# Feature-major queries and keys, and an earlier S5 part, in the first mixer of a two-layer decoder trunk

## Chip, cores and metric

One core of one Trainium2 chip. The metric is the device time in microseconds (us) of one execution. Engines: PE multiplies matrices (PEld is its weight load), DVE, ACT and POOL work element by element, SP issues the loads. Each engine takes its own instructions in the program's order, and waits for others by semaphores.

## What is computed

A trunk of two layers on 256 rows of width 1024, all in float32. The lines that matter here:

```
x = x + 0.5 * swiglu(rmsnorm(x))                      (first feed-forward stage)
proj = rmsnorm(x) @ w_in                              (first mixer)
u, c_q, c_kv, k_rope = split(proj, 512, 384, 256, 32)
s5 = gelu(S5(u)) gated by sigmoid(gelu(S5(u)) @ w_glu + b)
q = rmsnorm(c_q) @ w_uq        8 heads of 64 plain + 32 rotated columns
k, v = rmsnorm(c_kv) @ w_ukv   8 heads of 64 + 64; all heads share the rotated k_rope
o = causal_attention(q, k, v)
x = x + concat(s5, o) @ w_out
x = x + 0.5 * swiglu(...); x = x + 0.5 * swiglu(...)
x = x + differential_attention(rmsnorm(x)); x = x + 0.5 * swiglu(...); rmsnorm(x)
```

S5 is a diagonal state space: per group of 16 channels and each of 64 states a complex recurrence runs over the rows.

## The kernel before

The program runs in stages one after the other: feed-forward 0, first mixer (`mixer0`), feed-forward 1 and 2, second mixer, feed-forward 3, final norm. A build-time scheduler fixes each engine's order from the order of the code and from priorities; at run time nothing is moved.

**Weights.** `Weights` (L31 to L86) loads every weight in pieces of 128 x 1024 (512 KB) through SP into five `stage` buffers. ACT casts a piece to a high half (`whi`, L71), DVE subtracts to get the low half (`wlo`, L72), and each product is three products of halves. `mix0` (L165) is the list in which the first mixer's weights are loaded.

**Feed-forward 0** (`ffn`, L287) goes through 22 chunks `f` of the hidden width. PE computes chunk `f`'s gate and up products (`gu`, L318 in this stage), ACT and DVE make the hidden piece `hs`, and two chunks later PE multiplies it down into `acc` (L335). The hidden pieces of the first two chunks are turned by PE (`hT`, L367), the second of them right after chunk 2. Between the chunks this stage also runs a background generator, four steps a chunk at first, with all that later stages need and that does not depend on x: `rope_tables` (L491; cosines and sines from the positions, by range reduction `rtk`, `rtr` in `sincos`, then eighteen small DVE operations into `cc`, `ss`), the constants of the mixers (`lp`, `le`, `lw`: a scalar of the second mixer, by a power on POOL), and the S5 matrices (`s5_prep`; `w_re`, `w_im`, `tmat`). The lines of `rope_tables` that the change goes on from:

```
for t in range(2):
    for (cc, ss, o, h) in ((cc0, ss0, 0, 16), (cc1, ss1, 16, 8)):
        ...
        nc.vector.tensor_copy(out=cc[:, t, :h], in_=c)
        ...
        nc.vector.tensor_copy(out=ss[:, t, h:], in_=s)
```

**The first mixer** projects in the order queries' latent `cq`, keys' and values' latent `ckv`, S5 input `pu` (L732). Latents are normalised and turned into `cqh`, `cql`, `ckh`, `ckl`. `queries` makes q with the rows on the partitions (`pq`, 384 columns for four heads), POOL rotates 32 columns of each head (`rope`, L520), and `heads_turned` turns every head of q and k by PE (L935, 32 transposes), so that `scores` (L948, L949) can contract over 96 features. `u` is turned and spread into blocks, `block_inputs` (L886, L887) and `states` compute the S5 states on DVE (`z_re`, `z_im`, two scans, `xs_re`) and partly on POOL (`xs_im`, L918), and `outputs` (L991 to L993) makes `yp` from them. `attend(h)` issues the scores of head h + 2, then transposes head h's probabilities (`pt`, L763, copied to `pT` by ACT, L765) and multiplies them with v (`po`). The output products `attended` on `acc` (L743) start after head 6.

## Time and profile before

| | |
|---|---|
| runs | 1046.18, 1046.80, 1046.37 us (median 1046.37) |
| profiled execution | 1037.45 us, of it 1035.7 us span |
| granted clock, mean | 0.984 of full speed |
| PE busy | 1007.7 us (97%) |
| feed-forward 0 | 0 to 227 us |
| first mixer, PE's part | 227.3 us (first transposes of y) to 350.5 us; the gate's product `pz` starts at 327.3 |

The span runs from the first to the last instruction of the profiled execution. All times "at" below are us from its start. Busy time of PE is modelled: what a product costs is read from the distance of starts. An idle time in brackets is that before an instruction on its own engine, with what ended it.

### The profile page before, as it was taken

How to read it: one execution, taken by the hardware profiler on the slowest of the kernel's cores; microseconds unless marked ns; L12 is line 12 of the kernel's file. 1: busy time of each engine (PE TensorE's matmuls, PEld its weight loads, DVE VectorE, ACT ScalarE, POOL GpSimd, SP SyncE). 2: the span in 40 equal slices, each digit the busy share in tenths (PEclk: the TensorE clock that was granted, in tenths of full speed). 3: DMA queues.
4: the chain of work that ended last, by engine and by line, in shares of the span. 5: the costliest groups of instructions: out<-in, count | busy, mean ns of one | idle time of the engine just before them, and what ended most of it. 6: DMA issues, size and time to landing. Idle time of an engine off the chain costs nothing.

```text
span 1035.7 us, 15225 instructions
## 1 busy us (share of the span) xinstructions
PE 1007.7 (97%) x5796; PEld 878.4 (85%) x5796; DVE 677.4 (65%) x1251; ACT 545.3 (53%) x978; POOL 83.8 (8%) x109
## 2 busy tenths in 40 slices
PE   9999997999979999999999999999999999999997
PEld 7999996989868888888888888888888888888885
DVE  5789778366777885555558555554757777655543
ACT  5444442365636665555447455553567766555542
POOL 2110006600520000000000000000001000000000
PEclk9999999899969999999999999999999999999999
DMA  8766663134213596555628655564453448556521
GB/s 261 250 198 189 203 186 120 52 117 169 82 41 96 177 317 204 184 183 183 207 79 266 201 183 184 187 193 147 140 185 115 142 143 294 184 188 192 190 80 41
DMA packets 49802, 174.83 MB, mean 169 GB/s; under 512 B 6081, under 2 KB 7105, under 8 KB 49730
## 3 DMA queue, kind: packets, MB, share of 16 engines
q1 hardware_dynamic: 48576, 170.20, 51.2%
q10 hardware_dynamic: 1154, 3.67, 1.1%
q8 instruction: 45, 0.74, 0.3%
q14 instruction: 27, 0.22, 0.1%
HBM read 172.80 MB, written 1.05 MB: 168 GB/s over the span
## 4 chain that ended last, share of the span: by engine, by line
PE 85%; DVE 7%; ACT 3%; issue 2%; DMA 1%; POOL 1%; POOLq 0%; ACTq 0%; DVEq 0%; SPq 0%
PE acc L335 22%; PE gu L302 21%; PE gu L304 10%; PE gu L318 10%; PE proj L732 6%; PE gt L355 3%; PE acc L743 3%; DVE wlo L72 1%; DMA stage<-in_wff_dram 1%; PE pt L197 1%; PE pu L732 1%; DVE tmat L125 1%; PE ckv L732 1%; PE pz L1024 1%; PE cq L732 1%
## 5 line engine op out<-in xcount | busy, mean ns | idle before, releaser
L72 DVE TENSOR_TENSOR wlo<-stage,whi 128x1024 fp32r<-128x1024 f32 (+1 forms) x236 | 284.2, 1214 | 189.1 <-ACT whi L71 189.0
L302 PE MATMUL gu<-y,whi 128*128 128x512 f32 x960 | 341.6, 398 | 0.0
L71 ACT CAST whi<-stage 128x1024 fp32r<-128x1024 f32 (+1 forms) x236 | 241.0, 1032 | 126.9 <-PE gu L302 67.0
L304 PE MATMUL gu<-y,wlo 128*128 128x256 f32 x960 | 269.5, 281 | 0.0
L302 PEld LDWEIGHTS gu<-y,whi 128*128 128x128 f32 x960 | 180.4, 188 | 43.9
L335 PE MATMUL acc<-dhi,hs 128*128 128x512 f32 x704 | 193.1, 392 | 1.1 <-DVE hs L125 0.8
L304 PEld LDWEIGHTS gu<-y,wlo 128*128 128x128 f32 x960 | 181.4, 189 | 2.1
L335 PEld LDWEIGHTS acc<-dhi,hs 128*128 128x128 f32 x704 | 126.4, 188 | 28.1 <-DVE hs L125 2.3
L71 ACT CAST dhi<-stage 128x1024 fp32r<-128x1024 f32 x88 | 92.1, 1048 | 67.0 <-DMA stage<-in_wff_dram 66.8
L72 DVE TENSOR_TENSOR dlo<-stage,dhi 128x1024 fp32r<-128x1024 f32 x88 | 108.4, 1232 | 22.6 <-ACT dhi L71 22.4
L318 PE MATMUL gu<-y,whi 128*128 128x256 f32 x640 | 117.5, 285 | 0.0
L335 PE MATMUL acc<-dlo,hs 128*128 128x512 f32 x352 | 110.6, 390 | 0.0
L318 PEld LDWEIGHTS gu<-y,whi 128*128 128x128 f32 x640 | 102.0, 194 | 1.3
L318 PE MATMUL gu<-y,wlo 128*128 128x256 f32 x320 | 91.2, 285 | 0.0
L125 DVE TENSOR_TENSOR both<-gu,both 128x256 f32<-128x256 f32 x120 | 50.5, 421 | 47.2 <-ACT both L305 47.2
L305 ACT COPY both<-gu 128x256 f32<-128x256 f32 x120 | 44.4, 370 | 66.4 <-PE gu L304 66.4
L335 PEld LDWEIGHTS acc<-dlo,hs 128*128 128x128 f32 x352 | 66.1, 188 | 14.3
L134 ACT CAST hs<-sh 128x256 fp32r<-128x256 f32 x80 | 32.5, 406 | 66.2 <-DVE sh L125 66.1
L732 PE MATMUL proj<-whi,y 128*128 128x512 f32 x192 | 62.6, 396 | 0.2 <-ACT y L134 0.2
L318 PEld LDWEIGHTS gu<-y,wlo 128*128 128x128 f32 x320 | 62.0, 194 | 0.2 <-DVE wlo L72 0.2
L177 POOL TENSOR_TENSOR rs<-rs,mhalf 128x1 f32<-128x1 f32 x14 | 7.7, 553 | 668.6 <-DVE rs L131 668.6
L355 PE MATMUL gt<-whi,y 128*128 128x256 f32 x256 | 49.9, 289 | 0.8 <-ACT y L134 0.7
(330 smaller groups left out, 1221.5 us busy)
## 6 DMA issues: line engine op xcount, KB each, us to landing
stage<-in_wff_dram SPq DMA_DIRECT2D x264, 512.0 KB, 4.6
stage<-in_w_in_dram SPq DMA_DIRECT2D x24, 512.0 KB, 4.6
stage<-in_w_out_dram SPq DMA_DIRECT2D x16, 512.0 KB, 3.8
gain<-in_gains_dram ACTq DMA_DIRECT2D x6, 512.0 KB, 4.8
stage<-in_w_u_dram SPq DMA_DIRECT2D x4, 512.0 KB, 4.1
xr<-in_x_dram SPq DMA_DIRECT2D x2, 512.0 KB, 5.0
stage<-in_w_cq_dram SPq DMA_DIRECT2D x2, 512.0 KB, 3.7
stage<-in_w_ckv_dram SPq DMA_DIRECT2D x2, 512.0 KB, 4.6
```

The lines of the kernel that those rows point to most:

```text
L71: nc.scalar.copy(out=hi[:, c:c + w], in_=t[:, :w])
L72: nc.vector.tensor_tensor(out=lo[:, c:c + w], in0=t[:, :w], in1=hi[:, c:c + w].bitcast(F32), op=ALU.subtract)
L125: return nc.vector.tensor_tensor(out=out, in0=a, in1=b, op=op)
L134: copy = nc.scalar.copy(out=hi, in_=src)
L302: nc.tensor.matmul(gu, gh[:, k, s, :], y2[:, k].rearrange("p s c -> p (s c)"), start=k == 0, stop=False)
L304: nc.tensor.matmul(gu[:, :SEQ], gl[:, k, s, :], yh[:, k, :], start=False, stop=k == KT - 1)
L305: nc.scalar.copy(out=both[:, s], in_=gu[:, SEQ:])
L318: nc.tensor.matmul(gu[:, s * 256:(s + 1) * 256], w[:, k, s, :], a[:, k, :], start=(k == 0 and n == 0), stop=(k == KT - 1 and n == 2))
L335: nc.tensor.matmul(acc[t][c], a[:, sl], w[:, c * 512:(c + 1) * 512], start=(f == 0 and n == 0), stop=(f == NF - 1 and n == 2))
L355: last = nc.tensor.matmul(o, a[:, k, sl], w[:, k * 256:(k + 1) * 256], start=(k0 == 0 and n == 0), stop=(k0 > 0 and n == 11))
L732: last = nc.tensor.matmul(acc, a[:, k0 + k, sl], w[:, k * width:(k + 1) * width], start=(k0 == 0 and n == 0), stop=(k0 + per == nk and n = ...
L743: mm = nc.tensor.matmul(acc[t][c], a[:, k0 + k, sl], w[:, o:o + 512], start=(first and k == 0 and n == 0), stop=(last and k == 1 and n == 2))
```

## The change

1. **First mixer, u first.** `mix0` and the projections go `u`, `cq`, `ckv`. `u_blocks` runs between the two halves of `cq`, `block_inputs` between those of `ckv`; `states` has more stops (`step`), which are spread between the later parts, and `xs_im` is computed on DVE.
2. **Feature-major queries and keys.** The query weights are cut at 768 columns and each head is padded from 96 to 128 columns: 64 plain, 32 rotated, and the same 32 with halves swapped (three casts and three subtractions a piece). `queries` and `keys` produce features on the partitions, 256 rows wide; one DVE multiplication by a table `qtab` of ones, cosines and sines does the rotation, and the scores contract over 128. `heads_turned` goes, as do the rotations on POOL; the shared key part is rotated once on POOL (`key_rotation`) and turned (two transposes of `kd`).
3. **The table.** `rope_tables` ends with two DVE copies into `ct`, two PE transposes of it and an ACT copy into `qtab`.
4. **Attention's output products** are issued in four parts between heads 4 to 7; `attend` transposes head h before it issues the next scores; `gelu` is cut in two.

```diff
+    @staticmethod
+    def step(spec):
+        return 768 if spec[1] == "queries" else 1024
...
-                                    op=ALU.subtract)
+            parts = [(hi[:, c:c + w], lo[:, c:c + w], t[:, :w])]
+            if wide == "queries":
+
+                rows = slice(c // 96, (c + w) // 96)
+                h, l = (a[:, :1536].rearrange("p (r d) -> p r d", d=128)[:, rows] for a in (hi, lo))
+                v = t[:, :w].rearrange("p (r d) -> p r d", d=96)
+                parts = [(h[:, :, :96], l[:, :, :96], v)]
+                parts += [(h[:, :, a:a + 16], l[:, :, a:a + 16], v[:, :, b:b + 16]) for a, b in ((96, 80), (112, 64))]
+            for h, l, v in parts:
+                nc.scalar.copy(out=h, in_=v)
+                nc.vector.tensor_tensor(out=l, in0=v, in1=h.bitcast(F32), op=ALU.subtract)
...
-    mix0 = [(w, True) for w in (w_cq[0], w_cq[1], w_ckv[0], w_ckv[1], w_u[0], w_u[1], w_uq[0], w_ukv[0], w_uq[1],
-                                w_ukv[1], w_out0[2], w_glu, w_out0[3], w_out0[0], w_out0[1])]
+    mix0 = [(w, True) for w in (w_u[0], w_u[1], w_cq[0], w_cq[1], w_ckv[0], w_ckv[1])]
+    mix0 += [(w_uq[0], "queries"), (w_ukv[0], True), (w_uq[1], "queries"), (w_ukv[1], True)]
+    mix0 += [(w, True) for w in (w_out0[2], w_glu, w_out0[3], w_out0[0], w_out0[1])]
...
+        ct = s2("ct", [128, 2, 128])
+        nc.gpsimd.memset(ct[:, :, :64], 1.0)
+        nc.vector.tensor_copy(out=ct[:, :, 64:96], in_=cc0)
+        nc.vector.tensor_copy(out=ct[:, :, 96:], in_=ss0)
+        pt = bank("pt")[:, :SEQ]
+        for t in range(2):
+            nc.tensor.transpose(pt[:, t * 128:(t + 1) * 128], ct[:, t], ident)
+        nc.scalar.copy(out=qtab, in_=pt)
...
-        cq = [bank("cq")[:, :384] for _ in range(2)]
+
+        pu = [bank("pu") for _ in range(2)]
         c0, c1 = queue.pop(0), queue.pop(0)
-        product(cq[0], 0, c0, 0, 4, 384, yh, yl, KT)
+        product(pu[0], 0, c0, 0, 4, 512, yh, yl, KT)
         finish()
...
-        def project(acc, width, between):
-            for b in range(2):
-                w = queue.pop(0)
-                for t in range(2):
-                    product(acc[t], t, w, 4 * b, 4, width, yh, yl, KT)
-                more()
-                if b == 0:
-                    between()
...
-        ckv = [bank("ckv")[:, :288] for _ in range(2)]
-        project(ckv, 288, lambda: None)
-        cky = [low_rank(ckv[t][:, :256], 256, qg[:, 384:]) for t in range(2)]
...
-        def latents():
-            for t in range(2):
-                transpose_split(cqy[t], 3, cqh, cql, t)
-            for t in range(2):
-                transpose_split(cky[t], 2, ckh, ckl, t)
-
-        project(pu, 512, latents)
...
+        def project(acc, b, width):
+            w = queue.pop(0)
+            for t in range(2):
+                product(acc[t], t, w, 4 * b, 4, width, yh, yl, KT)
+            more()
...
+            kd, a, b = (s2(n, [128, 2, m]) for n, m in (("kd", 128), ("ka", 32), ("kb", 32)))
...
+            op(a, kp, cc0, MUL)
+            op(b[:, :, :16], kp[:, :, 16:], ss0[:, :, :16], MUL)
+            op(b[:, :, 16:], kp[:, :, :16], ss0[:, :, 16:], MUL)
+            op(kd[:, :, 64:96], a, b, ADD)
+            nc.gpsimd.tensor_copy(out=kd[:, :, 96:], in_=kd[:, :, 64:96])
+            return kd
...
         def queries(g):
-            w = queue.pop(0)
-            h = slice(4 * g, 4 * g + 4)
-            pq = [bank("pq")[:, :384] for _ in range(2)]
+
+            wh, wl = (w[:, :1536].rearrange("p (k h d) -> p k h d", k=3, h=4) for w in queue.pop(0))
+            for b in range(2):
+                pq = bank("pq").rearrange("p (h c) -> p h c", h=2)
+                for j in range(2):
+                    for n, (k, w, a) in enumerate(highs_first(range(3), wh, wl, cqh, cql)):
+                        nc.tensor.matmul(pq[:, j], w[:, k, 2 * b + j], a[:, k, :], start=n == 0, stop=n == 8)
+                h = 4 * g + 2 * b
+                tt(qT[:, h:h + 2, :], pq, qtab.unsqueeze(1).to_broadcast([128, 2, SEQ]), MUL)
+            more()
...
+        def keys(g):
...
+            for j in range(2):
+                for n, (k, w, a) in enumerate(highs_first(range(2), wh, wl, ckh, ckl)):
+                    nc.tensor.matmul(pk[:, j], w[:, k, 0, 128 * j:128 * j + 128], a[:, k, :], start=n == 0,
+                                     stop=n == 5)
+            for r in range(2):
+                nc.scalar.copy(out=kT[:64, 4 * g + r:4 * g + 4:2, :], in_=pk[64 * r:64 * r + 64])
...
+        def key_values(g):
...
             for t in range(2):
-                product(pq[t], t, w, 0, 3, 384, cqh, cql, 3)
-                nc.scalar.copy(out=q_sb[t][:, h, :], in_=pq[t].rearrange("p (h d) -> p h d", h=4))
-                rope(q_sb[t][:, h, 64:96], 4, cc0[:, t, :], ss0[:, t, :], 16, nc.gpsimd)
...
-        def keys_values(g):
...
-                product(pk[t].rearrange("p s c -> p (s c)"), t, w, 0, 2, 512, ckh, ckl, 2)
-                nc.scalar.copy(out=kfull[t][:, h, 0:64], in_=pk[t][:, 0].rearrange("p (h d) -> p h d", h=4))
-                nc.scalar.copy(out=v_sb[:, t, 256 * g:256 * g + 256], in_=pk[t][:, 1])
...
-        queries(0)
-        for t in range(2):
-            kv = kpe[:, t:t + 1, :]
-            rope(kv, 1, cc0[:, t, :], ss0[:, t, :], 16, nc.gpsimd)
-            nc.gpsimd.tensor_copy(out=kfull[t][:, :, 64:96], in_=kv.to_broadcast([128, 8, 32]))
...
-        keys_values(0)
+                sl = slice(t * 128, (t + 1) * 128)
+                for n, (k, w, a) in enumerate(highs_first(range(2), wh, wl, ckh, ckl)):
+                    nc.tensor.matmul(pv[:, t], a[:, k, sl], w[:, k, 1, :], start=n == 0, stop=n == 5)
+            nc.scalar.copy(out=v_sb[:, :, 256 * g:256 * g + 256], in_=pv)
+            more()
...
+            for z, x, y, op in ((z_re, v_re, v_im, ADD), (z_im, v_im, v_re, SUB)):
+                tt(z, x, c, MUL)
+                tt(t1, y, s, MUL)
+                tt(z, z, t1, op)
+                yield
             scan(z_re)
...
-            t2 = s2("t2", sh)[:, :, a]
-            for out, x, y, op in ((xs_im[:, h, o], z_re[:, :, a], s[:, :, a], MUL), (t2, z_im[:, :, a], c[:, :, a], MUL),
-                                  (xs_im[:, h, o], xs_im[:, h, o], t2, ADD)):
-                nc.gpsimd.tensor_tensor(out=out, in0=x, in1=y, op=op)
-
-        v = [block_inputs(b) for b in range(2)]
-        st = [states(b, *v[b]) for b in range(2)]
+            for xs, x, y, op in ((xs_re, z_re, z_im, SUB), (xs_im, z_im, z_re, ADD)):
...
+        def step(b):
+            next(st[b], None)
+
+        cq, ckv = ([bank(n)[:, :w] for _ in range(2)] for n, w in (("cq", 384), ("ckv", 288)))
+        project(cq, 0, 384)
+        u_blocks()
+        project(cq, 1, 384)
+        cqy = [low_rank(cq[t], 384, qg[:, :384]) for t in range(2)]
+        project(ckv, 0, 288)
+        st.append(states(0, *block_inputs(0)))
+        step(0)
+        project(ckv, 1, 288)
+        cky = [low_rank(ckv[t][:, :256], 256, qg[:, 384:]) for t in range(2)]
+        kd = key_rotation()
+        for t in range(2):
+            transpose_split(cqy[t], 3, cqh, cql, t)
+        step(0)
+        st.append(states(1, *block_inputs(1)))
...
-        def heads_turned(g):
-            for t in range(2):
-                for src, dst in ((q_sb, qT), (kfull, kT)):
-                    pt = bank("pt").rearrange("p (k c) -> p k c", c=128)
-                    for k in range(4):
-                        nc.tensor.transpose(pt[:96, k, :], src[t][:, 4 * g + k, :], ident)
-                    d = dst[:96, 4 * g:4 * g + 4, t * 128:(t + 1) * 128]
-                    if src is q_sb:
-                        nc.vector.tensor_copy(out=d, in_=pt[:96])
-                    else:
-                        nc.scalar.copy(out=d, in_=pt[:96])
-
...
-            nc.tensor.matmul(sp[:, :128], qT[:96, h, :128], kT[:96, h, :128], start=True, stop=True)
-            nc.tensor.matmul(sp[:, 128:384], qT[:96, h, 128:], kT[:96, h, :], start=True, stop=True)
+            nc.tensor.matmul(sp[:, :128], qT[:, h, :128], kT[:, h, :128], start=True, stop=True)
+            nc.tensor.matmul(sp[:, 128:384], qT[:, h, 128:], kT[:, h, :], start=True, stop=True)
...
+        def attended(w, t, k0, start, ks=(0, 1)):
+            if start and 0 in ks:
                 acc[t] = [bank("acc") for _ in range(2)]
-            out_product(acc, t, w, oh, ol, k0, start, False)
...
         def attend(h):
+            pT = turned(sc.pop(h), pb)
             if h < 6:
                 sc[h + 2] = scores(h + 2)
-            values(h, sc.pop(h))
...
-        heads_turned(0)
-        sc = {0: scores(0), 1: scores(1)}
-        next(st[0])
+            values(h, pT)
...
+        queries(0)
...
+        pt = bank("pt")[:, :SEQ]
+        for t in range(2):
+            nc.tensor.transpose(pt[:, t * 128:(t + 1) * 128], kd[:, t], ident)
...
+        step(1)
+        keys(0)
+        step(0)
+        key_values(0)
+        sc[0], sc[1] = scores(0), scores(1)
+        step(1)
+        step(0)
         queries(1)
+        step(0)
         attend(0)
-        next(st[1])
-        keys_values(1)
+        step(1)
+        keys(1)
+        key_values(1)
         attend(1)
-        for _ in st[0]:
-            pass
-        heads_turned(1)
-        for _ in st[1]:
-            pass
-        more()
+        step(1)
         yp = outputs(0)
         attend(2)
...
+        step(1)
         attend(3)
         osb = normalised(0)
-        attend(4)
+        g0 = gelu(yp)
         yp = outputs(1)
         heads_out(0, osb)
-        more()
+        attend(4)
+        w2 = queue.pop(0)
+        attended(w2, 0, 0, True, (0,))
+        in_channels(0, g0)
         attend(5)
-        gelu(1, yp)
+        attended(w2, 0, 0, True, (1,))
+        g1 = gelu(yp)
+        attend(6)
+        attended(w2, 1, 0, True, (0,))
+        in_channels(1, g1)
+        attend(7)
         halves(gh, gl, gt)
-        attend(6)
-        w2 = queue.pop(0)
-        attended(w2, 0, 0, True)
-        attend(7)
-        attended(w2, 1, 0, True)
-        heads_out(1, normalised(1))
+        attended(w2, 1, 0, True, (1,))
+        osb = normalised(1)
+        heads_out(1, osb)
         more()
         glu()
         w = queue.pop(0)
```

**Where instructions stand.** PE around chunk 2's turn in feed-forward 0, before (`hT` is the turn, the `gu` ahead of it ends chunk 2, that behind it begins chunk 3):

```order
L318 MATMUL gu<-y_121,wlo 128x256
L367 MATMUL hT<-ident,he 128x128 [waits DVE_49]
L367 MATMUL hT<-ident,he 128x128
L318 MATMUL gu<-y_121,whi 128x256 [waits Activation_49]
L318 MATMUL gu<-y_121,whi 128x256
```

and in the change (L380 is L367 of before, L331 is L318):

```order
L331 MATMUL gu<-y_122,wlo 128x256
L380 MATMUL hT<-ident,he 128x128 [waits DVE_49]
L380 MATMUL hT<-ident,he 128x128
L534 MATMUL pt<-ident,ct 128x128 [waits DVE_49,Pool_49]
L534 MATMUL pt<-ident,ct 128x128
L331 MATMUL gu<-y_122,whi 128x256 [waits Activation_49]
L331 MATMUL gu<-y_122,whi 128x256
```

The two transposes of `ct` stand between the turn and chunk 3's first product, with a wait for DVE and one for POOL.

DVE at the table's steps, before (`sh` and `hs` belong to chunk 3, `rtk` and `rtr` to the tables' range reduction):

```order
L131 TENSOR_SCALAR rtkh<-rtkh 128x48 [waits DVE_49]
L125 TENSOR_TENSOR sh<-sh,gu 128x256 [waits Activation_49]
L125 TENSOR_TENSOR rtk<-rtk,rtkh 128x48 [waits DVE_49]
L128 SCALAR_TENSOR_TENSOR rtr<-rtkh,ang 128x48
L125 TENSOR_TENSOR le<-lw,lc 128x2 [waits Pool_49]
L72 TENSOR_TENSOR wlo<-stage,whi 128x1024 [waits DMAHW1_49]
L128 SCALAR_TENSOR_TENSOR rtr<-rtk,rtr 128x48 [waits DVE_49]
L125 TENSOR_TENSOR nlam<-le 128x1 [waits DVE_49]
L125 TENSOR_TENSOR hs<-sh,hs 128x256 [waits Activation_49]
L128 SCALAR_TENSOR_TENSOR rtr<-rtkh,rtr 128x48 [waits DVE_49]
```

and in the change, the same stretch, then the end of the tables' steps:

```order
L137 TENSOR_TENSOR rtk<-rtk,rtkh 128x48 [waits DVE_49]
L140 SCALAR_TENSOR_TENSOR rtr<-rtkh,ang 128x48
L137 TENSOR_TENSOR le<-lw,lc 128x2 [waits Pool_49]
L140 SCALAR_TENSOR_TENSOR rtr<-rtk,rtr 128x48 [waits DVE_49]
L137 TENSOR_TENSOR nlam<-le 128x1 [waits DVE_49]
L140 SCALAR_TENSOR_TENSOR rtr<-rtkh,rtr 128x48 [waits DVE_49]
L143 TENSOR_SCALAR nlam<-nlam 128x1 [waits DVE_49]
L140 SCALAR_TENSOR_TENSOR rtr<-rtk,rtr 128x48 [waits DVE_49]
```

```order
L524 COPY cc_98<-co 128x8
L525 COPY cc_98<-co 128x8
L526 TENSOR_SCALAR ss_99<-si 128x8
L527 COPY ss_99<-si 128x8
L530 COPY ct<-cc_96 128x2x32 [waits DVE_49]
L531 COPY ct<-ss_97 128x2x32
L85 TENSOR_TENSOR wlo<-stage,whi 128x1024 [waits DMAHW1_49,PE_49,Activation_49]
L137 TENSOR_TENSOR sh<-sh,gu 128x256 [waits Activation_49]
L85 TENSOR_TENSOR wlo<-stage,whi 128x1024 [waits DMAHW2_49,Activation_49]
L137 TENSOR_TENSOR hs<-sh,hs 128x256 [waits Activation_49]
```

Chunk 3's `sh` and `hs` stood in the middle of the range reduction; now they stand behind all of it, behind the eighteen copies and behind both copies into `ct`.

ACT ahead of the keys' product in the mixer, before (`ckh` is the halved latent from which keys and values are made):

```order
L810 COPY kpe<-ckv 128x32 [waits DVE_49] x2
L71 CAST whi<-stage 128x1024 [waits DMAHW4_49,PE_49,Activation_49]
L71 CAST whi<-stage 128x128 [waits DMAHW5_49]
L134 CAST cqh<-pt 128x3x128 [waits PE_49] x2
L134 CAST ckh<-pt 128x2x128 [waits PE_49] x2
L824 COPY us<-pu 128x512 [waits PE_49]
```

and in the change:

```order
L146 CAST cqh<-pt 128x3x128 [waits PE_49] x2
L856 COPY kp<-ckv 128x32 [waits DVE_49]
L84 CAST whi<-stage 128x8x96 [waits DMAHW7_49,PE_49]
L84 CAST whi<-stage 128x8x16 x2
L84 CAST whi<-stage 128x4x96 [waits DMAHW0_49]
L84 CAST whi<-stage 128x4x16 x2
L146 CAST ckh<-pt 128x2x128 [waits PE_49,Pool_49]
L146 CAST ckh<-pt 128x2x128 [waits PE_49]
```

The six casts of the second query weight have come between `cqh` and `ckh`.

## Rows read from the trace of the kernel before

**Rows 1.** The page, section 1: busy time, share of the span and instructions of each engine
```profile
PE 1007.7 (97%) x5796; PEld 878.4 (85%) x5796; DVE 677.4 (65%) x1251; ACT 545.3 (53%) x978; POOL 83.8 (8%) x109
```

**Rows 2.** Windows; columns: stretch, then busy us of engines, granted clock (PEclk), DMA share, GB/s
```profile
20.00:168.00 148.00, 148.00 (x1066) 139.91 (x1064) 121.58 (x311) 71.57 (x103) 17.77 (x19) 1.00 0.64 200
168.00:178.00 10.00, 3.26 (x17) 2.23 (x15) 10.00 (x8) 0.89 (x2) 9.51 (x6) 0.95 0.52 147
178.00:190.00 12.00, 11.27 (x54) 11.30 (x55) 1.78 (x3) 2.70 (x4) 2.26 (x3) 0.50 0.14 49
293.00:306.00 13.00, 12.52 (x56) 12.24 (x57) 7.81 (x15) 2.84 (x7) 1.53 (x1) 0.50 0.26 82
```

**Rows 3.** Timeline of PE, first feed-forward stage; columns: start us, length us, line, operation
```profile
32.60 0.48 PE L318 MATMUL gu<-y,whi 128*128 128x256 f32 x2
...
34.11 0.40 PE L318 MATMUL gu<-y,whi 128*128 128x256 f32 x2
...
34.47 0.40 PE L318 MATMUL gu<-y,whi 128*128 128x256 f32 x2
```

**Rows 4.** Timeline of DVE beside it; in brackets idle time before and its releaser
```profile
40.71 0.29 DVE L125 TENSOR_TENSOR lp<-lv 128x128 f32<-128x128 f32 x1 [1.49 <-DMA lv<-in_lamv_dram]
...
44.94 0.16 DVE L125 TENSOR_TENSOR le<-lw,lc 128x2 f32<-128x2 f32 x1 [2.62 <-POOL lw L436]
...
50.29 0.17 DVE L128 SCALAR_TENSOR_TENSOR s5r<-s5kh,s5sc 128x16 f32<-128x16 f32 x1
50.49 0.18 DVE L128 SCALAR_TENSOR_TENSOR s5r<-s5k,s5r 128x16 f32<-128x16 f32 x1
...
52.10 0.20 DVE L125 TENSOR_TENSOR co<-co 128x48 f32<-128x48 f32 x1
...
53.43 0.17 DVE L511 COPY ss<-si 128x8 f32<-128x8 f32 x1
...
54.59 0.28 DVE L125 TENSOR_TENSOR s5sc<-s5sc 128x16 f32<-128x16 f32 x2 [0.28 <-ACT s5sc L427]
```

**Rows 5.** Timeline of POOL beside it
```profile
41.27 2.98 POOL L436 TENSOR_TENSOR s5w<-euler,s5t 128x16 f32<-128x16 f32 x1 [19.15 <-DVE s5t L125]
44.22 0.69 POOL L436 TENSOR_TENSOR lw<-euler,le 128x2 f32<-128x2 f32 x1
```

**Rows 6.** Timeline of PE, the products that follow the setup's long waits
```profile
187.47 0.77 PE L318 MATMUL gu<-y,whi 128*128 128x256 f32 x2
...
190.61 0.29 PE L318 MATMUL gu<-y,wlo 128*128 128x256 f32 x1
```

**Rows 7.** Timeline of PE, the mixer's first output product of the S5 part
```profile
287.64 0.43 PE L991 MATMUL yp<-u,tmat 128*128 128x64 f32 x2 [0.47 <-DVE t L125]
293.48 0.69 PE L992 MATMUL yp<-xs_re,w_re 128*128 128x64 f32 x2 [5.40 <-DVE xs_re L125]
...
306.65 0.35 PE L964 MATMUL po<-v_sb,pT 128*128 128x64 f32 x2
```

**Rows 8.** Timeline of PE, queries (pq) and turned heads (L935)
```profile
258.60 0.33 PE L732 MATMUL pq<-whi,cqh 128*128 128x384 f32 x1
...
260.16 1.03 PE L861 MATMUL pt<-ident,us 128*128 128x128 f32 x8
...
271.25 0.60 PE L935 MATMUL pt<-ident,q_sb 128*96 128x128 f32 x4
271.68 0.60 PE L935 MATMUL pt<-ident,kfull 128*96 128x128 f32 x4
```

**Rows 9.** Groups by line and shape, ACT, 225 to 355 us: count, busy us, mean ns
```profile
L71 ACT CAST whi<-stage 128x1024 fp32r<-128x1024 f32 x24 | 24.6, 1047 | 6.3 <-PE ckv L732 2.3 <-PE cq L732 1.6 <-PE pu L732 1.3
L71 ACT CAST whi<-stage 128x128 fp32r<-128x128 f32 x4 | 1.2, 294 | 0.0
```

**Rows 10.** Timeline of DVE in the mixer, a state product beside POOL's and one alone
```profile
285.25 1.74 DVE L125 TENSOR_TENSOR t<-z_im,sinn 128x504 f32<-128x504 f32 x1
...
296.26 0.67 DVE L125 TENSOR_TENSOR t<-z_im,sinn 128x504 f32<-128x504 f32 x1
```

More of the change, by code (lines that the diff above doesn't have):

```diff
@@ L734, in product, with out_product @@
         return last.ins
-    def out_product(acc, t, ws, hi, lo, k0, first, last):
+    def out_product(acc, t, ws, hi, lo, k0, first, last, ks=(0, 1)):
         wh, wl = ws
         sl = slice(t * 128, (t + 1) * 128)
-        for k in range(2):
+        for k in ks:
             for n, (w, a) in enumerate(three(wh, wl, hi, lo)):
@@ L824, in mixer0, with u_blocks @@
             nc.scalar.copy(out=us[t], in_=pu[t])
-        q_sb = [s4("q_sb", [128, 8, 96]) for _ in range(2)]
-        kfull = [s4("kfull", [128, 8, 96]) for _ in range(2)]
+        uT = s4("uT", [128, 4, 4, NBLK])
+        u = s4("u", [128, NPAIR, NBLK])
+        def u_blocks():
+            for t in range(2):
+                pt = bank("pt").rearrange("p (k c) -> p k c", c=128)
+                for k in range(4):
+                    nc.tensor.transpose(pt[:, k, :], us[t][:, k * 128:(k + 1) * 128], ident)
+                pv = pt.rearrange("p m (n i) -> p m i n", i=4)
+                for i in range(4):
+                    nc.scalar.copy(out=uT[:, :, i, 32 * t:32 * t + 32], in_=pv[:, :, i, :])
+            uv = u.rearrange("p (m a) n -> p m a n", a=4)
+            for a in range(4):
+                for i in range(4):
+                    dst = uv[32 * i:32 * i + 32, :, a, :]
+                    src = uT[32 * a:32 * a + 32, :, i, :]
+                    if i == 3 or i == 1 and a % 2:
+                        nc.scalar.copy(out=dst, in_=src)
+                    else:
+                        nc.vector.tensor_copy(out=dst, in_=src)
@@ new lines, in mixer0, with key_rotation, op @@
+        cqh, cql = s4("cqh", [128, 3, SEQ], F32R), s4("cql", [128, 3, SEQ], F32R)
+        ckh, ckl = s2("ckh", [128, 2, SEQ], F32R), s2("ckl", [128, 2, SEQ], F32R)
+        def project(acc, b, width):
[3 more added lines that the diff above has]
+            more()
+        def key_rotation():
+            kd, a, b = (s2(n, [128, 2, m]) for n, m in (("kd", 128), ("ka", 32), ("kb", 32)))
+            kp = s2("kp", [128, 2, 32])
+            for t in range(2):
+                nc.scalar.copy(out=kp[:, t], in_=ckv[t][:, 256:288])
+            def op(out, x0, x1, o):
+                nc.gpsimd.tensor_tensor(out=out, in0=x0, in1=x1, op=o)
+            nc.gpsimd.memset(kd[:, :, :64], 0.0)
+            op(a, kp, cc0, MUL)
[4 more added lines that the diff above has]
+            return kd
@@ L865, in mixer0 @@
-        u = s4("u", [128, NPAIR, NBLK])
-        uv = u.rearrange("p (m a) n -> p m a n", a=4)
-        for a in range(4):
-            for i in range(4):
-                dst = uv[32 * i:32 * i + 32, :, a, :]
-                src = uT[32 * a:32 * a + 32, :, i, :]
-                if i == 3 or i == 1 and a % 2:
-                    nc.scalar.copy(out=dst, in_=src)
-                else:
-                    nc.vector.tensor_copy(out=dst, in_=src)
-        keys_values(0)
+            wh, wl = (w[:, :1536].rearrange("p (k h d) -> p k h d", k=3, h=4) for w in queue.pop(0))
@@ L955, in scores, with values @@
             return s
-        def values(h, s):
+        def values(h, pT):
             g, k = divmod(h, 4)
@@ L994, in outputs, with gelu, in_channels @@
             return yp
-        def gelu(b, yp):
-            q, w = s2("gq", [128, 8, NBLK]), s2("gw", [128, 8, NBLK])
-            nc.scalar.activation(out=q, in_=yp, func=AF.Square)
-            ts(q, q, 0.044715, 1.0, MUL, ADD)
-            tt(w, q, yp, MUL)
+        def gelu(yp):
+            q, w, y = (s2(n, [128, 8, NBLK]) for n in ("gq", "gw", "gy"))
+            nc.scalar.copy(out=y, in_=yp)
+            nc.scalar.activation(out=q, in_=yp, func=AF.Square, scale=math.sqrt(0.044715))
+            stt(w, q, 1.0, y, ADD, MUL)
             nc.scalar.activation(out=w, in_=w, func=AF.Tanh, scale=math.sqrt(2.0 / math.pi))
-            stt(q, w, 1.0, yp, ADD, MUL)
+            stt(q, w, 1.0, y, ADD, MUL)
+            return q
+        def in_channels(b, q):
             gv = gt.rearrange("p m (n i) -> p m n i", i=4)
@@ L1045, in mixer0 @@
-        heads_turned(0)
-        sc = {0: scores(0), 1: scores(1)}
-        next(st[0])
+            values(h, pT)
+        queries(0)
+        for t in range(2):
+            transpose_split(cky[t], 2, ckh, ckl, t)
+        pt = bank("pt")[:, :SEQ]
+        for t in range(2):
+            nc.tensor.transpose(pt[:, t * 128:(t + 1) * 128], kd[:, t], ident)
+        for g in range(2):
+            nc.scalar.copy(out=kT[64:, 4 * g:4 * g + 4, :], in_=pt[64:].unsqueeze(1).to_broadcast([64, 4, SEQ]))
```

64 lines of the change are left out of this document (19 added, 45 removed).

## The prediction

> **What bounds the kernel now.** I read the page's busy times first: PE is busy for 1007.7 of 1035.7 us [rows 1], so time can only be won where PE idles or runs slowly, and time is lost wherever PE is made to wait. Then a table of stretches [rows 2], for the two stages that the change touches. In feed-forward 0 PE is busy in all of the 148 us from 20 to 168, at full clock: nothing there can take up a delay. [...]
>
> **The mixer, removed and added.** Time here is won in three terms.
> (a) The waits of 0.47 and 5.40 us at `yp` go if the states come earlier: u is first now, and DVE's state steps start with the first block while `ckv` is still being projected. -5.9 us.
> (b) Without that pause the half clock behind it goes. PE runs from 293.48 to 306.65 [rows 7] at 0.50 [rows 2], 13.2 us for what takes half of that at full clock: -6.6 us.
> (c) PE's work. Nine query products of 384 columns take 1.56 us (258.60 to 260.16, rows 8: 0.173 each); 36 of them, 6.2 us, become 72 of 256 columns, of which three start within 0.36 us [rows 3], 0.12 each: 8.6 us, +2.4. The 32 turned heads take 0.43 us for four [rows 8]: -3.5. The turn of `kd` adds two, +0.2. Keys and values go from 24 products of 512 columns to 48 of 256, the same columns: taken as equal. Together -0.9 us.
> [...]
>
> Against these stand new waits. `ckh`, without which keys and values can't start, now stands on ACT behind six casts of a query weight. A cast of 1024 columns takes 1.05 us and one of 128 takes 0.29 [rows 9]; between them I put 0.83 for the 768 columns and 0.51 for the 384, and at most 0.29 for each of the four small ones: 2.5 us; I take 2.2, since one cast begins before the last has ended. The copy `pT` of the first head stands behind two casts of an output weight, 2.1 us [rows 9], of which the next scores cover some: 1.5. For the new order of transposes, outputs and projections between the later heads, which no row of before shows, I take 0.8. Sum +4.5 us; bounds 0 (all of it covered) and 11 (twice this, and another 2 for the casts of gelu's new copy).
>
> What I cost at nothing: the three state operations that move to DVE, twice. They take 0.67 us each when POOL is still (1.74 beside POOL, rows 10), 4.0 us in all, on an engine that by its order then finishes the first block about 1.5 us before PE asks for it; without that cover each us late is a us on PE (a rival below). The three casts and subtractions a piece on ACT and DVE beside `cq` and `ckv`: these engines have room there, apart from the place above. SP issues as many pieces as before, u's first, in a part with DMA share well under one (0.26 over 293 to 306, rows 2). POOL loses the rotations of queries and `xs_im` and gains `key_rotation`, some six operations that run while PE makes the first queries. The split `attended` does the same 24 products, earlier.
>
> Mixer: -5.9 - 6.6 - 0.9 + 4.5 = **-8.9 us**, with bounds -13.4 and about -2.
>
> **The table, in feed-forward 0.** Two small transposes cost 0.2 us of work. Their place costs more. They stand on PE between chunk 2's turn and chunk 3's first product, and wait for DVE's second copy into `ct`. All that stands behind them on PE, chunk 3's `gu` and the eighteen chunks after it, waits with them. So: when can `ct` be ready? In before DVE's way there has two fixed posts. `lp` waits for a load until 40.71, and `le` waits for POOL's power until 44.94 [rows 4], because POOL does a power of 2.98 us from 41.27 and then its own from 44.22 [rows 5]. Both belong to other constants, but stand in DVE's order ahead of the tables' range reduction, and both hang on loads and constants, not on PE, so they come no earlier and no later in the change. From 44.94: five `rtr` and the clamp, each needing the last, at 0.20 (50.29 to 50.49, rows 4), 1.2; ACT's sine and cosine, 0.3 (DVE's idle of 0.28 at 54.59 for the same pair on S5's angles, rows 4); eighteen copies, 52.10 to the end of the last at 53.60 [rows 4], 1.5; two copies into `ct` with a dependence ahead, 0.4. That is 48.4; two transposes, and chunk 3 begins at 48.6 and not at 32.60 [rows 3]: **+16.0 us**, bounds 15 and 17 (a cast of 1.05 us [rows 9] may stand ahead of the sine on ACT).
>
> While PE waits, DVE and ACT soon wait too, since chunk 3's `sh` stands behind `ct` on DVE and the next weights need buffers that PE holds. They use some of the time for the tables, but they were not late afterwards: PE never waited for them up to 168. The stop at 168 to 178 is made by DVE and POOL [rows 2] on S5 matrices whose first products PE delivers at about 160, so it moves along whole.
>
> Then the clock. After the stop at 168 to 178 PE is at 0.50, and chunk products that follow run at half pace from 187.47 (0.77 for two, against 0.40 in rows 3) until 190.61 [rows 6]: 3.1 us, of which 1.6 lost. A pause of 16 us should do the same to chunk 3: **+1.6 us**; bounds 0 and 6.6, term (b), the longest stretch at half clock here.
>
> **Sum.** +16.0 + 1.6 - 8.9 = +8.7 us. The profiled execution took 1037.45 us, so it would take 1046.2 with a span of about 1044.4. The runs' median is 1046.37, 8.9 us above the profiled one; I carry the difference over one to one: **1055.1 us**. A difference of 0.2%, 2.1 us, is about the least that a measurement of this kernel can tell from none.
>
> **Rivals.**
> *The transposes don't hold PE (faster).* `ct` depends on positions alone. If it were ready when the turn ends, or if PE went on with chunk 3 meanwhile, only 0.2 us of the second part would be left: 1046.4 - 8.9 + 0.2 = 1037.7 us. It decides below a wait of about 7 us (with the clock's 1.6 it balances the mixer's gain), that is, with `ct` ready before 40; the load at 40.71 and the power at 44.22 [rows 4, 5] speak against it, and every row of PE here comes in the program's order. Chance 0.13.
> [...] No row here shows a product passing one that waits.
> *The mixer gives almost nothing.* DVE, now with `xs_im` and between weights' subtractions, is late again at `yp` by a few us, PE pauses, and the clock falls as before: term (b) is lost. 1046.4 + 17.6 - 2.3 = 1061.7 us. For it speaks the thin margin of 1.5 us, against it that POOL no longer slows DVE's operations [rows 10]. Chance 0.15.
> *The mixer gives all of it.* No new wait, and the clock rises at once in chunk 3: 1046.4 + 16.0 - 13.4 = 1049.0 us. Chance 0.12.
>
> **How the numbers follow.** The forecast, with its own range of 1052 to 1059, has 0.60. The range reaches out to the last two rivals, 1048.5 to 1062.5; left out are the first rival and a little at both ends. Faster comes from the first rival alone, 0.13; within 0.2% lies only a mixer at its best with a shorter wait, 0.02; slower 0.85.
>
> **What would show it.** In the profile after: a wait of some 15.8 us of PE for DVE's copy into `ct`, at about 32.6, at the line of the table's transposes; a granted clock of 0.50 for some 3 us behind it; the stop at 168 to 178 unchanged in length, but some 17 us later; in the mixer no wait over 2 us at `yp`, full clock throughout, and from the first turn of y to the gate's product 91 us in place of 100. The prediction is wrong if PE shows no such wait in feed-forward 0, or if the mixer's stretch comes out below 86 or above 98 us.

## The result, and the profile after

The change takes 1048.01 us, the median of 15 runs (1043.03 to 1050.44); before, 1043.93 us, the median of 15 runs (1036.56 to 1046.80; the three on which the prediction was made are among them, and are long ones). The ratio is 1.0053, interval 1.0029 to 1.0076: slower, by 0.5%, as forecast, but by less than the 8.7 us of the forecast: 4.1 us between the medians, 5.5 us by the ratio. In the traces it is more: span 1045.1 us against 1035.7, +9.4, where the working gave +8.7. So there are two things to explain: the trace, which came out as worked out, and the runs, which did not.

Busy times and count, section 1 of the page of the change (before: [rows 1]):

```profile
PE 1004.2 (96%) x5828; PEld 876.2 (84%) x5828; DVE 677.0 (65%) x1265; ACT 548.1 (52%) x981; POOL 64.9 (6%) x84
```

Timeline of PE in the change, in feed-forward 0 (before: [rows 3]; the bracket is the idle time before, with its releaser):

```profile
32.70 0.38 PE L380 MATMUL hT<-ident,he 128*128 128x128 f32 x2
49.21 0.66 PE L534 MATMUL pt<-ident,ct 128*128 128x128 f32 x2 [16.12 <-DVE ct L531]
49.52 0.78 PE L331 MATMUL gu<-y,whi 128*128 128x256 f32 x2
...
52.62 0.40 PE L331 MATMUL gu<-y,whi 128*128 128x256 f32 x2
```

PE reaches the table's transposes at once behind the turn and waits 16.12 us for DVE's second copy into `ct`. Chunk 3 begins at 49.52 and not at 32.60: 16.9 us later. DVE beside it (before: [rows 4]):

```profile
41.36 0.29 DVE L137 TENSOR_TENSOR lp<-lv 128x128 f32<-128x128 f32 x1 [1.91 <-DMA lv<-in_lamv_dram]
...
45.58 0.16 DVE L137 TENSOR_TENSOR le<-lw,lc 128x2 f32<-128x2 f32 x1 [1.82 <-POOL lw L449]
...
48.88 0.18 DVE L531 COPY ct<-ss 128x64 f32<-128x64 f32 x1
57.78 1.23 DVE L85 TENSOR_TENSOR wlo<-stage,whi 128x1024 fp32r<-128x1024 f32 x1 [8.72 <-ACT whi L84]
```

The two posts stand where they stood, 0.65 us later each: the load of `lv` at 41.36, POOL's power at 45.58. From there to the end of the last copy it is 3.5 us, as in the working. Then DVE waits 8.72 us for ACT's cast of the next weight, and ACT for 6.42 of them waits for PE's products of the late chunk 3: the pause goes on through ACT to DVE. Stretches of the change (columns as in [rows 2]):

```profile
32.00:49.00 17.00, 1.08 (x10) 0.85 (x8) 11.00 (x54) 6.35 (x10) 3.64 (x2) 0.60 0.73 259
36.00:49.00 13.00, 0.00 (x0) 0.00 (x0) 8.86 (x52) 3.13 (x6) 3.64 (x2) 0.50 0.65 215
49.00:54.00 5.00, 4.79 (x29) 4.82 (x30) 0.06 (x1) 0.37 (x1) 0.00 (x0) 0.67 0.02 3
50.00:52.00 2.00, 2.00 (x11) 2.00 (x10) 0.00 (x0) 0.28 (x1) 0.00 (x0) 0.50 0.04 8
54.00:168.00 114.00, 114.00 (x801) 107.15 (x801) 86.84 (x226) 47.70 (x70) 3.93 (x9) 1.00 0.56 174
290.00:295.00 5.00, 4.40 (x23) 4.08 (x22) 4.48 (x11) 2.09 (x4) 0.00 (x0) 0.66 0.63 206
295.00:340.00 45.00, 40.90 (x305) 36.81 (x306) 35.33 (x98) 29.07 (x69) 0.00 (x0) 1.00 0.19 60
```

The clock falls to 0.50 in the pause, the first products of chunk 3 run at half pace, 0.78 for two in place of 0.40, until 52.6, and from 54 to 168 PE is full again, 114.00 of 114, so nothing is given back there. The stop in the S5 setup comes some 18 us later than in before (the first turn of `w_im` in it at 189.15 and not at 171.18), and PE waits 5.9 us in it, against 5.7 to 7.5 in the four traces of before (three of them come below). In the mixer there is one short stretch of half clock (290 to 295, mean 0.66), and none behind `yp`. PE's waits in the mixer, in us: in total, times, longest:

```profile
PE po L992 <- ACT pT L789: 3.5, 6, 1.2
PE pk L888 <- ACT ckh L146: 1.5, 1, 1.5
...
PE pv L899 <- DVE ckl L137: 0.6, 1, 0.6
PE pt L1010 <- DVE osb L137: 0.5, 1, 0.5
```

The wait for `xs_re` has gone; `ckh` and `ckl` are waited for, and `pT` oftener. In before it was:

```profile
PE po L964 <- ACT pT L765: 1.5, 2, 0.9
```

By stage, from the first turn of y in the mixer and the first turn of y in the next stage (half clock: sum over stretches of 1 us of PE's busy time times one less the granted clock):

| trace | span | to the mixer | mixer | rest | lost at half clock, S5 setup | lost at half clock, mixer |
|---|---|---|---|---|---|---|
| before | 1035.7 | 227.3 | 123.2 | 685.2 | 6.0 | 6.6 |
| the change | 1045.1 | 245.7 | 115.4 | 684.1 | 7.8 | 1.6 |
| difference | +9.4 | +18.4 | -7.8 | -1.1 | +1.8 | -5.0 |

Among the four traces of before the way to the mixer lies between 226.9 and 228.3 us, so a difference of about 1 us there says nothing.

### The profile page after: what moved, and what is told of

The parts are those of the page before. It is cut to its first block, busy times and chain, and to the rows that moved or that the text cites. A ratio compares the mean times of both kernels' runs of the same rounds, so it can differ in the third digit from the quotient of the medians.

```text
span 1045.1 us, 15276 instructions
## 1 busy us (share of the span) xinstructions
PE 1004.2 (96%) x5828; PEld 876.2 (84%) x5828; DVE 677.0 (65%) x1265; ACT 548.1 (52%) x981; POOL 64.9 (6%) x84
## 4 chain that ended last, share of the span: by engine, by line
PE 81%; DVE 7%; issue 3%; ACT 2%; DMA 2%; POOL 0%; POOLq 0%; DVEq 0%; ACTq 0%
PE acc L348 22%; PE gu L315 20%; PE gu L317 10%; PE gu L331 10%; PE proj L756 6%; PE acc L767 2%; DVE wlo L85 2%; DMA stage<-in_wff_dram 2%; PE pu L756 1%; PE gt L368 1%; PE cq L756 1%; ACT whi L84 1%; DVE tmat L137 1%; PE pq L878 1%; PE pt L210 1%
## 5 line engine op out<-in xcount | busy, mean ns | idle before, releaser
L85 DVE TENSOR_TENSOR wlo<-stage,whi 128x1024 fp32r<-128x1024 f32 (+3 forms) x244 | 284.7, 1179 | 198.7 <-ACT whi L84 198.3
L84 ACT CAST whi<-stage 128x1024 fp32r<-128x1024 f32 (+3 forms) x244 | 241.8, 1007 | 137.6 <-PE gu L315 66.3
L331 PE MATMUL gu<-y,whi 128*128 128x256 f32 x640 | 119.0, 288 | 0.0
L331 PEld LDWEIGHTS gu<-y,whi 128*128 128x128 f32 x640 | 103.3, 196 | 1.3
L331 PE MATMUL gu<-y,wlo 128*128 128x256 f32 x320 | 91.8, 287 | 0.0
L318 ACT COPY both<-gu 128x256 f32<-128x256 f32 x120 | 44.4, 370 | 65.8 <-PE gu L317 65.8
L331 PEld LDWEIGHTS gu<-y,wlo 128*128 128x128 f32 x320 | 62.7, 196 | 0.0
```

What stands on the lines that cost most here:

```text
L84: nc.scalar.copy(out=h, in_=v)
L85: nc.vector.tensor_tensor(out=l, in0=v, in1=h.bitcast(F32), op=ALU.subtract)
L318: nc.scalar.copy(out=both[:, s], in_=gu[:, SEQ:])
L331: nc.tensor.matmul(gu[:, s * 256:(s + 1) * 256], w[:, k, s, :], a[:, k, :], start=(k == 0 and n == 0), stop=(k == KT - 1 and n == 2))
```

## Experiments

Theory: the table's place on PE costs its wait and the clock behind it, and the mixer wins what the traces show. First rival: the wait is partly paid back later. Since runs and traces disagreed by half, a second question went along: where do before's runs, 1034 to 1050 us, differ from one another?

**before_table and late_table: the wait alone, and the change without it.** The first puts the table, at the same place, into the kernel before; the second moves the turn of the table in the change behind the first thirteen steps of the S5 setup (`n` counts from 0). The edit of the second, in the lines that matter:

```diff
+    ct = cst.tile([128, 2, 128], F32, name="ct")
...
-        ct = s2("ct", [128, 2, 128])
         nc.gpsimd.memset(ct[:, :, :64], 1.0)
...
+    def table_turned():
         pt = bank("pt")[:, :SEQ]
...
-        yield from s5_prep()
+        for n, _ in enumerate(s5_prep()):
+            if n == 12:
+                table_turned()
+            yield
```

Expected of before_table:

> The kernel before with the table alone: memset, two copies into ct, two transposes on PE and the copy into qtab, which nothing reads. Theory (the table's place on PE costs its full wait and the clock behind it, and nothing gives it back): PE waits 15 to 17 us for ct at about 32.6, the clock is 0.50 for some 3 us after it, span 17 to 18 us above that of before's trace of 1035.7, so 1053 to 1054, and the timed runs 1.6% to 1.7% slower than before. Rival (the runs of before carry a loss of several us that a pause in feed-forward 0 takes away, which is why the change cost 4 to 5 us in the runs and 9 in the traces): the wait is there, but the runs are only 0.9% to 1.3% slower.

Measured: ratio 1.0192, interval 1.0141 to 1.0244; 1062.62 us median of 6 runs, 1055.93 to 1064.84. PE's wait in its trace:

```profile
PE pt L520 <- DVE ct L517: 16.1, 1, 16.1
```

Its way to the mixer is 245.7 us, 18.4 more than before's, the same as in the change. That is the theory's 17 to 18 and a little. But its span is 1063.1, 9 us more than expected, and those 9 us stand in its mixer, 132.1 us for 123.2, where nothing was edited. PE lay there at half clock for 37.5 us, against 17.1 in before's trace; most of it is in this stretch:

```profile
310.00:347.00 37.00, 34.46 (x154) 32.83 (x154) 20.75 (x54) 11.68 (x31) 2.82 (x2) 0.51 0.17 58
```

The rival falls: the interval lies above its 0.9% to 1.3%, and in the trace nothing is paid back.

Expected of late_table:

> The changed kernel with ct kept in its own buffer and the two transposes issued after twelve steps of the S5 setup, some three chunks later; the mixer as in the change. Theory: ct has long been ready, PE does not wait, the table costs 0.2 us; 17.8 us less than the change, span 1027 to 1028, and 0.8% to 0.9% faster than before: what the mixer alone gives. Rival (the wait is paid back by something later, so taking it out wins less): span 1030 to 1036, runs within 0.4% of before.

Measured: ratio 0.9897, interval 0.9853 to 0.9942; 1031.2 us median of 6 runs, 1025.21 to 1031.90; span 1029.4. The table's transposes in its trace:

```profile
60.52 0.38 PE L536 MATMUL pt<-ident,ct 128*128 128x128 f32 x2
60.66 0.48 PE L331 MATMUL gu<-y,whi 128*128 128x256 f32 x2
```

They take 0.14 us and wait for nothing; the way to the mixer is 228.4 us, and the mixer is the change's, 115.4. Theory held in the main: the loss of the change is the place of two transposes, and without it the change gains 1%. The span is 1.4 us above the expected 1028; among the parts, the S5 setup lost 8.4 us at half clock, where the change lost 7.8.

**before_again, before_third, before_fourth: the kernel before, three more traces.** No edit.

> The kernel before once more, for a second trace. Its runs lie between 1036.6 and 1046.8 us, and the first trace at 1037.45. Theory (the spread is a matter of single executions, at certain places): this execution lies somewhere in that span, and where it is more than 2 us longer than the first, the table of stretches shows the difference at one or two places, behind a pause of PE by the clock, or at the start. Rival: the difference is spread evenly over the program.

> The kernel before, for a trace of one of its long executions. Theory (what makes them long is half clock in the mixer, behind the wait for xs_re): if it comes out above 1043 us, PE lies at half clock for over 25 us behind that wait, with a loss of over 12 us there, and the rest is as in the short ones; if it comes out under 1040, for 14 to 18 us. Rival: the long ones lose their time elsewhere, at the S5 setup's waits or evenly.

> The same as before_third: one more execution of the kernel before, read the same way.

The first two came out at 1039.43 and 1039.48 us, with mixers of 123.6 and 123.7 us; the third at 1044.98, a long one, with 131.7. The stretch behind the wait for `xs_re`, in the trace of before that the prediction was made on:

```profile
290.00:307.00 17.00, 13.52 (x61) 13.06 (x61) 10.98 (x19) 3.84 (x8) 3.23 (x3) 0.51 0.20 63
307.00:327.00 20.00, 19.06 (x135) 16.52 (x134) 16.31 (x54) 12.73 (x36) 0.00 (x0) 1.00 0.17 54
```

and in before_fourth:

```profile
290.00:307.00 17.00, 13.84 (x61) 13.37 (x62) 10.96 (x21) 3.94 (x8) 2.92 (x3) 0.50 0.18 63
307.00:327.00 20.00, 19.38 (x88) 18.47 (x88) 10.26 (x34) 7.38 (x22) 0.00 (x0) 0.51 0.15 53
```

The instructions, their order and the wait (5.40 and 5.41 us) are the same. In the first the clock is back after 307; in the second it is at 0.51 to 327, and PE gets through 88 products in 20 us and not 135. By the sum of 1-us stretches 16.4 us are lost there against 6.6, and the gate's product starts at 335.34 and not at 327.26. The rest of the two traces is equal within 1 us (226.9 and 684.6 us). In these traces that is the difference of a short and a long execution, and the timed runs fit it: of 54 runs of before, 23 lie from 1033.6 to 1041.1 us and 31 from 1043.1 to 1049.6; where the granted clock is on record, its mean is 0.978 to 0.987 in the first and 0.971 to 0.978 in the second. The expected 12 us and more behind that wait were found; the rival (elsewhere, or evenly) falls. Why the clock is back after 17.1 us in one execution and after 37.5 in another no run shows.

**before_fill: the same wait, with the clock held.** 22 products of the identity fill PE's wait at `yp` (the trace records each as two):

```diff
                 nc.tensor.matmul(yp[:, q, :], tmat[:, k, :], u[:, k, :], start=True, stop=False)
+                if k == 0:
+                    idle = bank("idle")
+                    for _ in range(22):
+                        nc.tensor.matmul(idle[:, :128], ident, ident, start=True, stop=True)
```

> The kernel before with 22 products of the identity on PE behind the first S5 output product, in the wait for xs_re; they write a bank that nothing reads. The wait itself stays. Theory (the spread of before's runs, 1034 to 1048, is the time that PE stays at half clock behind this one wait: 17 us in the two traces of before, 37.5 us in that of before_table, and the change wins by taking it away): clock 1.00 through the mixer, span 6 to 7 us under that of before's short executions, 1029 to 1031, and the runs lie within 4 us, with none over 1036: against before 0.985 to 0.993. Rival (the clock falls and stays by something else, the narrow products of 64 columns): half clock behind the wait as before, runs spread as before's.

Measured: ratio 0.9988, interval 0.9963 to 1.0012. Not the gain expected; but 11 of its 12 runs lie from 1041.3 to 1044.0, between before's two groups. Its timeline of PE and its stretches:

```profile
287.54 5.13 PE L995 MATMUL idle<-ident 128*128 128x128 f32 x44
293.12 0.43 PE L996 MATMUL yp<-xs_re,w_re 128*128 128x64 f32 x2 [0.45 <-DVE xs_re L125]
...
304.37 0.33 PE L763 MATMUL pt<-ident,s 128*128 128x128 f32 x1 [2.36 <-ACT s L757]
...
307.97 0.69 PE L964 MATMUL po<-v_sb,pT 128*128 128x64 f32 x2 [2.67 <-ACT pT L765]
```

```profile
287.00:298.00 11.00, 10.28 (x90) 10.09 (x90) 11.00 (x16) 3.29 (x7) 4.45 (x3) 1.00 0.00 1
...
304.00:327.00 23.00, 19.79 (x90) 18.89 (x90) 9.74 (x35) 9.08 (x28) 0.00 (x0) 0.55 0.09 34
```

The clock stays at 1.00 through the wait and the five us of products of 64 columns behind it, as the theory has it for that place. Six us further PE runs into ACT, which is late: it waits 2.36 and 2.67 us for the heads' exponentials and copies, and there the clock falls, for 20.5 us. Half right: the wait for `xs_re` sets off the half clock, but before's mixer holds other waits behind it, and holding the clock at one of them led, in this trace, to the next. In the change the longest wait of the mixer is the 1.5 us for `ckh`.

**before_xs_dve and pool_states: which part takes the wait away.** The first moves only `xs_im` to DVE, in before's order; the second moves it back to POOL, in late_table.

```diff
-                nc.gpsimd.tensor_tensor(out=out, in0=x, in1=y, op=op)
+            tt(xs_im[:, h, o], z_re[:, :, a], s[:, :, a], MUL)
+            tt(t1, z_im[:, :, a], c[:, :, a], MUL)
+            tt(xs_im[:, h, o], xs_im[:, h, o], t1, ADD)
```

> The kernel before with xs_im on DVE, its order otherwise kept. Theory (the earlier start of the states takes the wait away, not the engine, as pool_states showed from the other side): the wait at yp stays between 3 and 7 us, and the half clock behind it stays. Rival (POOL slows DVE beside it, 1.74 us for 0.67, and without it the states are in time): the wait falls under 2 us and the clock stays at 1.00.

> late_table with xs_im computed on POOL again, as before. [...] Rival (the earlier start of the states is what matters, not the engine): no wait over 1 us at yp, within 1 us of late_table.

PE at `yp` in before_xs_dve:

```profile
290.22 0.43 PE L991 MATMUL yp<-xs_re,w_re 128*128 128x64 f32 x2 [2.01 <-DVE xs_re L125]
```

The wait goes from 5.40 to 2.01 us, the half clock behind it stays (13.7 us, 6.8 lost), the mixer takes 120.9 us: only 2.4 less, since the scores now wait 1.5 us for `qk` on DVE. In pool_states there is no wait at `yp` at all, and the mixer takes 117.0 us, 1.7 more than late_table's: the values' product waits 2.7 us for `ckl` on DVE, 2.1 more than there. DVE in pool_states, ahead of and behind the second block's scan of `z_im` (286.59, 1.22 us), which the last two of POOL's three products there wait for:

```profile
274.07 0.68 DVE L137 TENSOR_TENSOR xs_re<-xs_re,t 128x504 f32<-128x504 f32 x1
...
288.37 1.74 DVE L137 TENSOR_TENSOR t<-z_im,sinn 128x504 f32<-128x504 f32 x1
```

So neither expectation came out whole. With the rest of the change in place, the earlier order is enough without the engine; in before's order the engine alone takes away more than half of the wait; and of the two only the run with the change's order has no half clock behind `yp`. The order without the feature-major form was not run. (pool_states' whole time, 1027.23, is lower than late_table's by the S5 setup, where 2.5 us are lost to the clock and not 8.4; that place differs from trace to trace here, 2.5 to 8.8.)

**ckh_first: the mixer's new wait.** In late_table, the next weight is taken behind the latent's split:

```diff
         queries(0)
         for t in range(2):
             transpose_split(cky[t], 2, ckh, ckl, t)
+        more()
```

(and not at the end of `queries(0)`).

> late_table with the second query weight taken behind the latent's split, so that ckh stands ahead of five of the six casts on ACT. Theory (ckh waits for these casts): PE's wait for ckh falls from 1.5 to under 0.9 us, and the stretch of half clock near it, 3.4 us, goes; 1 to 3 us less in the mixer. Rival (it waits for its own transposes, or the casts then come late for the second queries): the wait stays, or as much appears at the second queries.

> ckh_first once more, timed: the changed mixer with the table turned later and the latent's split ahead of the query weight's casts. Theory (the table's wait, 17 to 18 us, and the mixer's new wait for ckh are gone, and the mixer's clock stays up): 1.2% to 1.5% faster than before, runs 1025 to 1031, closer together than before's. Rival (the gain of ckh_first's single trace was the S5 setup's clock by chance): not faster than late_table, 1.0%.

PE's waits in its mixer, and two stretches, the S5 setup's and the mixer:

```profile
PE po L995 <- ACT pT L791: 3.5, 6, 1.2
...
PE pk L891 <- ACT ckh L146: 0.5, 1, 0.5
```

```profile
168.00:195.00 27.00, 22.11 (x108) 20.33 (x108) 11.74 (x10) 3.68 (x7) 16.77 (x13) 0.62 0.26 79
227.00:317.00 90.00, 84.45 (x592) 76.99 (x592) 69.52 (x165) 53.84 (x130) 4.21 (x11) 1.00 0.27 86
```

The wait for `ckh` falls from 1.5 to 0.5 us, the one for `ckl` goes, and a new one of 0.5 us, for `qk`, comes up. The clock is 1.00 from 227 to 317, but that this comes of the shorter waits is not shown: late_fill, below, has late_table's waits for `ckh` and `ckl` and no half clock in its mixer either. The mixer takes 112.6 us, 2.8 less than late_table's. Timed: ratio 0.9839, interval 0.9786 to 0.9892; 1027.12 us median of 6 runs, 1023.62 to 1028.87, so 1.6%, a little over the expected 1.2% to 1.5%, which the interval covers. The runs lie within 5.3 us, before's beside them within 14.9. This version beats both kernels.

**late_fill: products in the S5 setup's waits.** 14 products of the identity ahead of each of the last two turns there, in late_table.

> late_table with 14 products of the identity on PE ahead of each of the two last turns of the S5 matrices in feed-forward 0, where PE waits 2.7 and 3.1 us for DVE. Theory (the clock falls for want of work there, and lies at 0.50 for 6.8 to 17 us in the traces, at a loss of 2.5 to 8.4 us): clock 1.00 there, 2 to 8 us less than late_table, runs 1023 to 1028. Rival (the fillers delay the turns, or the narrow products behind them let the clock fall all the same): within 1.5 us of late_table or slower.

Measured: ratio 0.9899, interval 0.9856 to 0.9942, the same as late_table, as the rival has it. It decides little for the theory, since the fillers missed the waits:

```profile
168.69 3.29 PE L692 MATMUL idle<-ident 128*128 128x128 f32 x28
...
179.09 1.09 PE L695 MATMUL pt<-ident,w_im 128*128 128x128 f32 x4 [6.67 <-DVE w_im L137]
```

The first fillers ran early, and PE then waited 6.67 us with nothing; the second ones ran at half clock, in 5.46 us. What was less at half clock (10.2 us of time and not 17) the fillers took themselves: the way to the mixer is 231.7 us, 3.3 more than late_table's. Its mixer, in which nothing was edited against late_table, has the same wait for `ckh`, and yet the clock stays up:

```profile
PE pk L894 <- ACT ckh L146: 1.5, 1, 1.5
```

```profile
231.00:346.00 115.00, 107.78 (x719) 96.83 (x719) 85.88 (x185) 65.16 (x147) 4.76 (x12) 1.00 0.34 108
```

It takes 114.2 us, 1.2 less than late_table's, and 1.6 more than that of ckh_first: so of ckh_first's 2.8 us some 1.2 can be the clock alone.

**out_whole: the split output products.** In ckh_first, the 24 products stand whole behind heads 6 and 7, as in before.

> ckh_first with the 24 products of the first output weight in two whole parts behind heads 6 and 7 again, as before the change. ckh_first takes 89.8 us from the first turn of y to the gate's product. Theory (the four parts fill PE's waits for pT between heads 4 and 7): the waits for pT grow by 1 to 4 us and the stretch with them, to 91 to 94 us. Rival (the heads' waits are short and the split only shifts work): within 1 us of 89.8.

Measured: 89.2 us from the turn to the gate's product, 112.0 to the next stage against 112.6. The rival held, in one trace of each: the split is worth nothing that shows.

## Why the parts were right and the sum was wrong

**The table's wait: right.** Worked out +16.0 us, bounds 15 to 17; it is 16.9, the excess being the load that both posts hang on (0.65 us later) and the step from the end of the last copy to chunk 3 (0.46 in place of 0.2). before_table shows it alone, late_table its absence. The products behind the transposes did not pass, nor did their weight loads: from 36 to 49 us PE ran no product and no weight load (0.00 and 0.00 in the row above). So the rival that the transposes don't hold PE is out.

**The clock behind it: right.** +1.6 worked out; 1.5 lost from 49 to 53.

**The mixer in the trace: near, term by term.** -8.9 worked out, -7.8 measured to the next stage; to the gate's product it is 92.6 us in place of 100.0, where 91 was named. Term (a), the waits of 0.47 and 5.40 us at `yp` [rows 7], is gone whole. Of term (b), 6.6, all went behind `yp` but 1.6 came back behind the new waits for `ckh` and `ckl`, where the working had full clock throughout. Term (c): the queries' products,

```profile
282.66 0.36 PE L878 MATMUL pq<-cqh,whi 128*128 128x256 f32 x1
...
287.05 0.60 PE L210 MATMUL pt<-ident,cy 128*128 128x128 f32 x4
```

36 in 4.39 us, are 0.122 us apart: the row's 0.120 [rows 3]. (The new form of queries and keys was not run by itself; what it does to PE's work is read from such rows alone.) New waits: 1.5 for `ckh` (2.2 expected), 0.6 for `ckl`, 0.5 for `osb`, and 2.0 more for `pT` (3.5 against 1.5 in before; 1.5 and 0.8 expected): 4.6 together, against 4.5. `xs_im` was ready at 305.7, 1.8 us before `yp` began at 307.5, where the working had a margin of 1.5, for which it shows no row. So the rival in which the mixer gives almost nothing is out. The figure of the rival in which it gives all, 1049.0, lies next to the measured 1048.01, but by chance: it has no new wait and no half clock in chunk 3, and the trace has 4.6 and 1.5 us.

**The step that failed** stands in the sum: "The runs' median is 1046.37, 8.9 us above the profiled one; I carry the difference over one to one". That difference was no constant of the measurement. The profiled execution was a short one of before, and the three runs were long ones; what lies between them is, by before_fourth's trace, time at half clock in the mixer, behind the wait for `xs_re`: the very thing that the change takes away. Term (b) was thus mis-sized for the runs: 6.6 us in the trace, and also in the other short executions (7.0), but 16.4 in a long one (before_fourth). By the spans the change is 9.4, 7.4 and 7.4 us slower than the three short executions, and 1.9 slower than before_fourth (1045.1 and 1043.2). The runs say the same. Of the 15 runs of before that were timed beside the change's, the seven short ones average 1038.3 us and the eight long ones 1045.6; the change's own, whose trace lacks that wait, average 1047.7, 13 of the 15 from 1046.9 to 1050.4: 9.4 and 2.1 us more, and together the measured 0.53%. Of the 7.1 us between the forecast of 1055.1 and the measured 1048.01, 4.6 are this difference (8.7 worked out, 4.1 between the medians); the other 2.4 are the base, three runs that happened to be long ones, 1046.37, where the median of 15 is 1043.93. Had the 8.9 us been taken whole for half clock behind that wait, the forecast would have stayed at the 1046.2 of the line before, 1.8 us under the measured time. A sign was there to see: the runs' median lay 8.9 us above the profiled execution, and PE's clock in a stretch of that trace was 0.50 behind a wait that was to go.

## What to carry to other kernels

An instruction of 0.1 us on an engine that is busy to the last can cost what its inputs are late, for all that stands behind it, as here, where two transposes (0.14 us in late_table) cost the change 16.9 us and 1.5 more at half clock: set it where its inputs have long been there, as late_table does, and read the order of the built program, not the code, for what it stands in front of. Before a difference is carried from one profiled execution to the runs, ask why the runs lie elsewhere: two clusters in the runs and a clock below 1.00 in the trace can mean, as here, that one place costs more in some executions than in others (6.6 and 16.4 us), and a change that takes this place away wins a different amount from each.
